# Copies of a bias made from DRAM to DRAM in an earlier layer, and rotary tables loaded into a free residual

## The chip, the cores and the metric

One core of a Trainium2 chip runs the whole program. TensorE (PE) multiplies, VectorE (DVE) and ScalarE (ACT) work on vectors, GpSimd (POOL) adds a little and issues some DMAs, SyncE (SP) issues most of the DMAs. The metric is the device time of one execution in microseconds.

## The reference

Two blocks of a network follow each other for 256 positions of width 1024. Block 1 is one layer of dilated attention and a state space scan with a feed-forward part. Block 2 has two layers on two streams, the target `x` and a context `xc`. Each layer is a feed-forward part, a mixer over both streams and a second feed-forward part. The mixer of layer 1 joins a latent attention (MLA) with rotary positions and a neighbourhood attention whose scores get a bias per head and per distance:

```python
for l in range(DEPTH_2):
    ...
    x = x + 0.5 * mx[2] * swiglu_2(modulate(rms_norm(x), mx[0], mx[1]), *ffn1)
    xc = xc + 0.5 * mc[2] * swiglu_2(modulate(rms_norm(xc), mc[0], mc[1]), *ffn1)
    h = modulate(rms_norm(x), mx[3], mx[4])
    hc = modulate(rms_norm(xc), mc[3], mc[4])
    ...            # l == 0: window and differential attention, l == 1: the one below
    x = x + mx[5] * y
    x = x + 0.5 * mx[8] * swiglu_2(modulate(rms_norm(x), mx[6], mx[7]), *ffn2)

# in mix_mla_neighbourhood (layer 1)
q_rope = apply_rope2d(rms_norm(q[..., C_NOPE:], qn_rope), cos, sin)
k_rope = apply_rope2d(rms_norm(k_rope, kn_rope), cos, sin)
# in neighbourhood_attention, for each of the 4 rows of 64 positions
bias = rpb_f[:, dr_idx[None, :, None], dc_idx[:, None, :]]
s = jnp.einsum('bqhd,bjkhd->bhqjk', q_row, k_band).astype(jnp.float32) * scale + bias
```

After layer 1's mixer the context is not needed any more, so its residual is last read by the norm ahead of that mixer.

## The kernel before

Activations lie with the features on the 128 partitions, as eight blocks of 128 x 256 for each stream. A linear unit multiplies one 128-wide slab of a weight matrix (512 KB, loaded by SP into one of five `wraw` buffers at L107) with all eight blocks. Weights and activations are each split into two parts (`wh`, `wl` by L114 and L115; `ah`, `al` by L355 and L356), and three products of the parts make one in full precision (L133 to L135). `K.run` goes through a list of units and emits loads and splits some units ahead; plain functions in the list, such as `tables`, are emitted where they stand, and `weave` spreads a list of such steps evenly between units. The order in which an engine takes its instructions is planned by the framework from the data that they need; each engine's queue is then fixed and is worked off in order.

A norm of a stream (`norm_stream`, with raised priority) is a chain: sums over PE (L330), mean on DVE (L314), root on ScalarE (L315), reciprocal on DVE (L316), spreading over PE (L338), and then for each block a product on DVE (L351), a cast with the shift on ScalarE (L355) and the remainder on DVE (L356).

The mixer of layer 1 is `mix_cd`. Its units are, in order: two of `cd_ckv` (indices 0 and 1), six of `cd_cq` for the target alone, one of `cd_kr` (index 8), four of `cd_dk` (9 to 12) and others. At its beginning ScalarE's queue loads the rotary tables `cos` and `sin` (96 x 256 each, L1397 and L1398) into temporary buffers, and `tables`, behind unit 4, scales them by the gains of queries and keys (L1093, L1094) into blocks 4 to 7 of `free`, the place of the context's residual `xc`. POOL's queue loads the bias rows of eight heads (889 elements each, `A["rpb"][:, 4:11]`) onto eight partitions of blocks 0 to 3 of `free` (L1402), and then writes 64 copies of them to the DRAM tensor `rpb` (L1404), from which the neighbourhood attention later reads a bias per head that is shifted by one element from row to row:

```python
    rows = free[:8, 0:4].rearrange("p a t -> p (a t)")[:, :7 * 127]
    nc.gpsimd.dma_start(rows, A["rpb"][:, 4:11].rearrange("h r c -> h (r c)"))
    rpb = K.dram.tile([64, 8, 7 * 127], F32, name="rpb")
    nc.gpsimd.dma_start(rpb.rearrange("q h u -> h q u"), rows.unsqueeze(1).to_broadcast([8, 64, 7 * 127]))
```

The same pattern stands at the start of block 1: the bias rows `brs` of eight partitions are written as 32 copies to the DRAM tensor `brow` (L474, 896 KB), and the load of `tri` (L478) and two mask loads `mk` (L500) stand behind it in the code. POOL's only arithmetic is the addition of a mask to the bias in the neighbourhood attention (L1597).

In layer 0, `block2` weaves 40 steps into the units of the first feed-forward part. Each step is one piece of the modulation (`K.pieces`): a load of 512 KB (`w_mod`) and two products on DVE (L981).

Of the kernel before, what the change touches and what calls it, by code (L numbers as in the profile page):

```python
# [8 lines left out]
F32 = mybir.dt.float32  # L9
# [1081 lines left out]
def rope_tables(K, c, s, cos, sin, gain, gain_sw, scale, rows):  # L1091
    nc = K.nc
    nc.vector.tensor_scalar(c[rows], cos[rows], gain[rows], scale, op0=ALU.mult, op1=ALU.mult)  # L1093
    nc.vector.tensor_scalar(s[rows], sin[rows], gain_sw[rows], scale, op0=ALU.mult, op1=ALU.mult)  # L1094
    return c[rows], s[rows]
# [8 lines left out]
def skew(work):  # L1104

    deep, out = max(len(w) for w in work), []
    for i in range(len(work) + deep - 1):
        for d in range(deep):
            if 0 <= i - d < len(work) and d < len(work[i - d]):
                out.append(work[i - d][d])  # L1110
    return out
# [17 lines left out]
def v_units(K, src, n, kpb, evac, last):  # L1129

    nc = K.nc
    nsl = -(-KB // kpb)

    def make(i):
        def f(s, slabs):
            for t in range(2):
                if t:
                    K.step()

                p = (K.pa.tile([128, 512], F32, name="pa") if i == last else K.psum())[:, :n]  # L1140
                for k in range(KB):
                    h, lo = slabs[k // kpb]
                    c = slice(k % kpb * n, (k % kpb + 1) * n)
                    ah, al = K.ACT[s][0][:, k, t * 128:(t + 1) * 128], K.ACT[s][1][:, k, t * 128:(t + 1) * 128]
                    nc.tensor.matmul(p, ah, h[:, c], start=k == 0, stop=False)  # L1145
                    nc.tensor.matmul(p, al, h[:, c], start=False, stop=False)
                    nc.tensor.matmul(p, ah, lo[:, c], start=False, stop=k == KB - 1)  # L1147
                evac(s, t, i, p)
        return Unit(src, i * nsl, nsl, f)

    return [make(i) for i in range(src.shape[0] // nsl)]


def out_proj(K, src, layer, streams, done, steps=()):
    def evac(m):
        return lambda s, p: K.residual(s, m, p, K.mod(layer, s, 5)(m), True)

    K.run(weave([K.lin(src, m, K.acts, evac(m)) for m in range(KB)], steps), streams, done=done)
# [232 lines left out]
def mix_cd(K, streams):  # L1391
    nc, A = K.nc, K.A
    ctx = ExitStack()
    ap = K.pool(ctx, "cd", 1)
    full, r96 = slice(0, 128), slice(0, 96)
    cos, sin = K.t1("cos"), K.t1("sin")
    nc.scalar.dma_start(cos[r96], A["mla_cos"])  # L1397
    nc.scalar.dma_start(sin[r96], A["mla_sin"])  # L1398
    sw_mask = [p ^ 8 for p in range(32)]
    free = K.X["c"]  # L1400
    rows = free[:8, 0:4].rearrange("p a t -> p (a t)")[:, :7 * 127]
    nc.gpsimd.dma_start(rows, A["rpb"][:, 4:11].rearrange("h r c -> h (r c)"))  # L1402
    rpb = K.dram.tile([64, 8, 7 * 127], F32, name="rpb")
    nc.gpsimd.dma_start(rpb.rearrange("q h u -> h q u"), rows.unsqueeze(1).to_broadcast([8, 64, 7 * 127]))  # L1404
    tabs = {}

    def tables():
        for n, k, at_ in (("q", "cq", 4), ("k", "ckr", 6)):
            c, s = rope_tables(K, free[:, at_], free[:, at_ + 1], cos, sin, K.col(k), K.col(k + "_sw"), 1.0, r96)
            tabs[n] = (c, s, sw_mask)  # L1410

    dqg = ap.tile([128, 1], F32, name="dqg")
# [25 lines left out]
    def latent(kind, b):  # L1438
        def evac(s, p):
            k = (kind, s)  # L1440
            nc.scalar.copy(raw[k][:, b], p)
            K.square_add(kind + s, raw[k][:, b], b == 0)
            if b + 1 == rank[k]:
                K.later(lambda: first(k))

        def first(k):
            r = K.rstd_cols(K.sums(k[0] + k[1]), 2, 1.0 / (128 * rank[k]), 1e-6)
            K.later(lambda: second(k, r))

        def second(k, r):  # L1450
            q = K.on_all(r)
            n = range(rank[k])
            K.norm(k[0], [raw[k][:, j] for j in n], lambda j: K.col("cq_a" if kind == "q" else "ckv_a", j), None,
                   *([t[:, j] for j in n] for t in parts[k]), q)

        return evac
# [58 lines left out]
    units = [K.lin(A["cd_ckv"], b, K.acts, latent("k", b)) for b in range(2)]  # L1515
# [6 lines left out]
    dq_units = [K.lin(A["cd_dq"], b, K.acts, dq_evac(b), streams=one) for b in range(4)]  # L1522
    units += dq_units[:2] + [vc_unit(i) for i in range(2)] + dq_units[2:]
    units += v_units(K, A["cd_dv"], 256, 4, vd_evac, 1)
    K.run(units[:5] + [tables] + units[5:-1], streams, ko=2)
    K.flush()
    tctx.close()

# [82 lines left out]
    steps = skew(work + [attend(b, scores_d, 1.0, vd, 4 + b) for b in range(4)])  # L1611
# [6 lines left out]
    ctx.close()  # L1618


def block2(K, layers=(0, 1)):
    nc, A = K.nc, K.A
    for layer in layers:
        both = ["c", "x"]

        def norms(i, layer=layer):
            return lambda s: K.norm_stream(s, K.mod(layer, s, i + 1), K.mod(layer, s, i))

        fctx = ExitStack()
        hid_p = K.pool(fctx, "h1", 14)  # L1630
        K.ffn(A[f"f1g{layer}"], A[f"f1u{layer}"], [A[f"f1d{layer}{i}"] for i in range(3)], both,
              lambda s, m: K.mod(layer, s, 2)(m), hid_p, K.pieces(40), norms(3))
        fctx.close()
        K.dbg(f"d_xf{layer}", K.X["x"])
        K.dbg(f"d_cf{layer}", K.X["c"])
        if layer == 0:
            mix_ab(K, both)
            out_proj(K, A["ab_out"], 0, both, norms(6))
            tail = both
        else:  # L1640
            while K.bg:
                K.background()
            K.mctx.close()
            mix_cd(K, both)
            out_proj(K, A["cd_out"], 1, ["x"], norms(6))
            tail = ["x"]
        K.dbg(f"d_xm{layer}", K.X["x"])
        K.dbg(f"d_cm{layer}", K.X["c"])
        fctx = ExitStack()
        hid_p = K.pool(fctx, "h2", 14)  # L1650

        def done(s):
            K.norm_stream(s, K.mod(1, s, 1), K.mod(1, s, 0))

        def after(s, m):
            if layer == 1:
                nc.sync.dma_start(A["out"][:, m], K.X["x"][:, m])

        K.ffn(A[f"f2g{layer}"], A[f"f2u{layer}"], [A[f"f2d{layer}{i}"] for i in range(3)], tail,
              lambda s, m: K.mod(layer, s, 8)(m), hid_p, K.pieces(40 if layer == 0 else 0),  # L1660
              done if layer == 0 else None, after)
        fctx.close()
        K.dbg(f"d_x2{layer}", K.X["x"])
# [3 lines left out]
def kernel(ctx, tc, A, parts=(1, 2)):  # L1667
# [24 lines left out]
    if 2 in parts:  # L1692
        for s in ("c", "x") if 1 not in parts else ():
            for b in range(KB):
                K.square_add(s, K.X[s][:, b], b == 0)
            K.norm_stream(s, K.mod(0, s, 1), K.mod(0, s, 0))
        block2(K)
    else:
        K.flush()
        nc.sync.dma_start(A["out"], K.X["x"])  # L1700
# [189 lines left out]
```

## Time and profile before

| | us |
|---|---|
| median of 3 runs | 2549.88 |
| lowest and highest run | 2544.33 and 2550.07 |
| the profiled execution | 2545.32 |
| its span, first to last instruction | 2543.5 |

Busy time is given for each engine; operations on one engine overlap a little at their ends. A row of a timeline gives the start, the duration, the engine, the line, the operation with its output and inputs and how many were merged, and in brackets the idle time of the engine before it and what ended that. ACTq and SPq are the queues of ScalarE and SP on which they issue DMAs. q0 is the DMA queue of POOL, q1 that of SP, and a queue's share is the time of its packets as a part of the time of all 16 DMA engines.

### The profile page before, as it was taken

What the parts mean: (1) busy time and instruction counts of PE and PEld (TensorE: products, weight loads), DVE (VectorE), ACT (ScalarE), POOL (GpSimd) and SP (SyncE); (2) the same over time, 40 slices, a digit from 0 to 9 for tenths busy, and PEclk for the clock granted to TensorE, in tenths of its full rate; (3) what the DMA queues carried; (4) which work ended last, traced back from release to release, by engine and by line L of the source; (5) the groups of instructions that cost most, each with busy time, mean ns of one, the idle gap of its engine ahead of it and who ended that gap; (6) DMA issues with size and microseconds to landing.
All of it is one profiled execution on the core that took longest, in us unless ns stands there. A gap on an engine that the chain in (4) does not pass through costs nothing.

```text
span 2543.5 us, 38370 instructions
## 1 busy us (share of the span) xinstructions
PE 2457.1 (97%) x15104; PEld 2122.3 (83%) x15104; DVE 1642.2 (65%) x3009; ACT 1070.2 (42%) x1934; POOL 15.4 (1%) x20
## 2 busy tenths in 40 slices
PE   6999999999999999999999999999999968999999
PEld 6999999999988888885598888888888857866999
DVE  4667777787867564767767666566545344667554
ACT  4657565535522222436743222243222234555443
POOL 0000000000000000000000000000000000000000
PEclk9999899999999999999999999999999988999999
DMA  8555455676455553431025545325555342232563
GB/s 227 148 156 161 144 163 182 210 246 203 162 166 167 164 168 99 130 98 51 1 75 178 170 150 170 128 91 178 171 166 164 103 96 74 98 95 82 172 185 125
DMA packets 117204, 363.66 MB, mean 143 GB/s; under 512 B 21050, under 2 KB 28730, under 8 KB 117024
## 3 DMA queue, kind: packets, MB, share of 16 engines
q1 hardware_dynamic: 114512, 355.73, 44.2%
q0 software_dynamic: 1008, 3.09, 1.0%
q10 hardware_dynamic: 1504, 2.40, 0.3%
q8 instruction: 119, 1.95, 0.3%
q14 instruction: 61, 0.50, 0.1%
HBM read 357.34 MB, written 3.82 MB: 142 GB/s over the span
## 4 chain that ended last, share of the span: by engine, by line
PE 70%; DVE 2%; DMA 2%; ACT 1%; issue 0%; ACTq 0%
PE pm L133 20%; PE pm L134 20%; PE pm L135 20%; PE pt L1120 1%; DMA sin<-mla_sin 1%; PE pa L1027 1%; PE pt L1051 1%; PE pa L1574 1%; PE pm L1319 1%; PE pm L1582 1%; PE pm L1259 0%; PE pa L1335 0%; PE pa L1296 0%; PE pm L1604 0%; PE pm L1145 0%; PE pa L1147 0%
## 5 line engine op out<-in xcount | busy, mean ns | idle before, releaser
L133 PE MATMUL pm<-ah,wh 128*128 128x256 f32 (+2 forms) x3096 | 1012.7, 329 | 46.4 <-ACT ah L355 35.6
L134 PE MATMUL pm<-al,wh 128*128 128x256 f32 (+2 forms) x3096 | 1007.1, 326 | 1.2 <-DVE al L356 1.1
L135 PE MATMUL pm<-ah,wl 128*128 128x256 f32 (+2 forms) x3096 | 1005.2, 325 | 0.0
L114 ACT CAST wh<-wraw 128x1024 fp32r<-128x1024 f32 (+4 forms) x535 | 540.3, 1013 | 1057.1 <-PE pm L134 850.0
L115 DVE TENSOR_TENSOR wl<-wraw,wh 128x1024 fp32r<-128x1024 f32 (+4 forms) x535 | 627.2, 1175 | 242.2 <-ACT wh L114 240.0
L133 PEld LDWEIGHTS pm<-ah,wh 128*128 128x128 f32 (+1 forms) x3096 | 588.6, 191 | 107.2 <-ACT ah L355 37.3
L134 PEld LDWEIGHTS pm<-al,wh 128*128 128x128 f32 (+1 forms) x3096 | 590.7, 191 | 54.2 <-issue 2.4
L135 PEld LDWEIGHTS pm<-ah,wl 128*128 128x128 f32 (+1 forms) x3096 | 590.6, 191 | 51.4 <-issue 1.7
L134 PE MATMUL pm<-hl,wh 128*128 128x512 f32 (+1 forms) x934 | 317.1, 339 | 0.0
L133 PE MATMUL pm<-hh,wh 128*128 128x512 f32 (+1 forms) x934 | 316.6, 339 | 0.0
L135 PE MATMUL pm<-hh,wl 128*128 128x512 f32 (+1 forms) x934 | 316.4, 339 | 0.0
L981 DVE SCALAR_TENSOR_TENSOR junk<-wraw,cactc 128x1024 f32<-128x1024 f32 x112 | 137.2, 1225 | 213.2 <-DMA wraw<-w_mod 212.8
L981 DVE SCALAR_TENSOR_TENSOR junk<-wraw,cactx 128x1024 f32<-128x1024 f32 x144 | 176.0, 1222 | 41.0 <-DMA wraw<-w_mod 38.6
L133 PEld LDWEIGHTS pm<-hh,wh 128*128 128x128 f32 x934 | 175.9, 188 | 21.2 <-issue 0.2
L135 PEld LDWEIGHTS pm<-hh,wl 128*128 128x128 f32 x934 | 175.9, 188 | 20.9
L134 PEld LDWEIGHTS pm<-hl,wh 128*128 128x128 f32 x934 | 175.9, 188 | 20.9
L119 ACT CAST hh<-g 128x512 fp32r<-128x512 f32 (+1 forms) x113 | 59.2, 526 | 162.1 <-DVE g L413 162.1
L413 DVE TENSOR_TENSOR g<-g,pm 128x512 f32<-128x512 f32 (+1 forms) x113 | 64.0, 566 | 58.7 <-PE pm L135 57.3
L120 DVE TENSOR_TENSOR hl<-g,hh 128x512 fp32r<-128x512 f32 (+1 forms) x113 | 63.8, 566 | 0.3
L409 ACT ACTIVATE g<-pm 128x512 f32<-128x512 f32 (+1 forms) x116 | 56.1, 489 | 2.5 <-PE pm L135 2.3
L443 DVE SCALAR_TENSOR_TENSOR xc<-pm,mcol0c,xc 128x256 f32<-128x256 f32 x56 | 26.9, 480 | 46.0 <-PE pm L135 45.8
L307 DVE TENSOR_TENSOR acc<-acc,sq 128x256 f32<-128x256 f32 x105 | 42.3, 419 | 13.7 <-ACT sq L306 13.4
(421 smaller groups left out, 2228.7 us busy)
## 6 DMA issues: line engine op xcount, KB each, us to landing
wraw<-w_mod SPq DMA_DIRECT2D x144, 512.0 KB, 4.1
wraw<-f1g SPq DMA_DIRECT2D x44, 512.0 KB, 3.7
wraw<-f1u SPq DMA_DIRECT2D x44, 512.0 KB, 4.2
wraw<-f2g SPq DMA_DIRECT2D x44, 512.0 KB, 3.7
wraw<-f2u SPq DMA_DIRECT2D x44, 512.0 KB, 4.0
wraw<-f1d SPq DMA_DIRECT2D x32, 512.0 KB, 4.0
wraw<-f2d SPq DMA_DIRECT2D x32, 512.0 KB, 3.7
wraw<-w_xbc SPq DMA_DIRECT2D x24, 512.0 KB, 3.6
```

The costliest lines, as they stand in the source:

```text
L114: nc.scalar.copy(h[:, :f], raw[:, :f])
L115: nc.vector.tensor_tensor(lo[:, :f], raw[:, :f], h[:, :f].bitcast(F32), op=ALU.subtract)
L119: self.nc.scalar.copy(h, src)
L120: self.nc.vector.tensor_tensor(lo, src, h.bitcast(F32), op=ALU.subtract)
L133: nc.tensor.matmul(out, h[:, c], ah, start=first, stop=False)
L134: nc.tensor.matmul(out, h[:, c], al, start=False, stop=False)
L135: nc.tensor.matmul(out, lo[:, c], ah, start=False, stop=last)
L307: nc.vector.tensor_tensor(self.acc[key], self.acc[key], sq, op=ALU.add)
L409: nc.scalar.activation(half(g["g"], s), p, AF.Silu)
L413: nc.vector.tensor_tensor(t, t, p, op=ALU.mult)
L443: self.nc.vector.scalar_tensor_tensor(x, p, gate, x, op0=ALU.mult, op1=ALU.add)
L981: nc.vector.scalar_tensor_tensor(junk, raw, 1.0, K.cact[s], op0=ALU.mult, op1=ALU.mult, accum_out=K.mcol[layer, s][:, j:j + 1])
```

## The change

The copies of the bias are made by eight DMAs, each of 8 x 8 rows straight from the input in DRAM to the DRAM tensor. They are emitted as steps 10 to 17 of the list that layer 0 weaves into its first feed-forward part, which then has 48 steps. They stand on POOL's queue as before. The load of the rows into `free` and the broadcast store in `mix_cd` go away. The rotary tables are loaded twice, as four DMAs on POOL's queue, straight into blocks 4 to 7 of `free`, and are scaled there in place. `tables` stands behind unit 8 and no longer behind unit 4.

```diff
--- before.py
+++ after.py
@@ -1393,20 +1393,17 @@
     ctx = ExitStack()
     ap = K.pool(ctx, "cd", 1)
     full, r96 = slice(0, 128), slice(0, 96)
-    cos, sin = K.t1("cos"), K.t1("sin")
-    nc.scalar.dma_start(cos[r96], A["mla_cos"])
-    nc.scalar.dma_start(sin[r96], A["mla_sin"])
     sw_mask = [p ^ 8 for p in range(32)]
     free = K.X["c"]
-    rows = free[:8, 0:4].rearrange("p a t -> p (a t)")[:, :7 * 127]
-    nc.gpsimd.dma_start(rows, A["rpb"][:, 4:11].rearrange("h r c -> h (r c)"))
-    rpb = K.dram.tile([64, 8, 7 * 127], F32, name="rpb")
-    nc.gpsimd.dma_start(rpb.rearrange("q h u -> h q u"), rows.unsqueeze(1).to_broadcast([8, 64, 7 * 127]))
+    for i, n in enumerate(("cos", "sin", "cos", "sin")):
+        nc.gpsimd.dma_start(free[r96, 4 + i], A["mla_" + n])
+    rpb = K.rpb
     tabs = {}
 
     def tables():
         for n, k, at_ in (("q", "cq", 4), ("k", "ckr", 6)):
-            c, s = rope_tables(K, free[:, at_], free[:, at_ + 1], cos, sin, K.col(k), K.col(k + "_sw"), 1.0, r96)
+            c, s = free[:, at_], free[:, at_ + 1]
+            c, s = rope_tables(K, c, s, c, s, K.col(k), K.col(k + "_sw"), 1.0, r96)
             tabs[n] = (c, s, sw_mask)
 
     dqg = ap.tile([128, 1], F32, name="dqg")
@@ -1522,7 +1519,7 @@
     dq_units = [K.lin(A["cd_dq"], b, K.acts, dq_evac(b), streams=one) for b in range(4)]
     units += dq_units[:2] + [vc_unit(i) for i in range(2)] + dq_units[2:]
     units += v_units(K, A["cd_dv"], 256, 4, vd_evac, 1)
-    K.run(units[:5] + [tables] + units[5:-1], streams, ko=2)
+    K.run(units[:9] + [tables] + units[9:-1], streams, ko=2)
     K.flush()
     tctx.close()
 
@@ -1618,6 +1615,13 @@
     ctx.close()
 
 
+def bias_rows(K):
+
+    K.rpb = K.dram.tile([64, 8, 7 * 127], F32, name="rpb")
+    rows = K.A["rpb"][:, 4:11].rearrange("h r c -> h (r c)").unsqueeze(0).to_broadcast([8, 8, 7 * 127])
+    return [lambda i=i: K.nc.gpsimd.dma_start(K.rpb[8 * i:8 * i + 8], rows) for i in range(8)]
+
+
 def block2(K, layers=(0, 1)):
     nc, A = K.nc, K.A
     for layer in layers:
@@ -1626,10 +1630,13 @@
         def norms(i, layer=layer):
             return lambda s: K.norm_stream(s, K.mod(layer, s, i + 1), K.mod(layer, s, i))
 
+        steps = K.pieces(40)
+        if layer == 0:
+            steps[10:10] = bias_rows(K)
         fctx = ExitStack()
         hid_p = K.pool(fctx, "h1", 14)
         K.ffn(A[f"f1g{layer}"], A[f"f1u{layer}"], [A[f"f1d{layer}{i}"] for i in range(3)], both,
-              lambda s, m: K.mod(layer, s, 2)(m), hid_p, K.pieces(40), norms(3))
+              lambda s, m: K.mod(layer, s, 2)(m), hid_p, steps, norms(3))
         fctx.close()
         K.dbg(f"d_xf{layer}", K.X["x"])
         K.dbg(f"d_cf{layer}", K.X["c"])
```

## Rows read from the trace of the kernel before

**Rows 1.** The page, part 1: busy time of each engine, share of the span.

```profile
PE 2457.1 (97%) x15104; PEld 2122.3 (83%) x15104; DVE 1642.2 (65%) x3009; ACT 1070.2 (42%) x1934; POOL 15.4 (1%) x20
```

**Rows 2.** Stretches: us, busy per engine (instructions), granted clock, DMA share, GB/s.

```profile
1050.00:1055.00 5.00, 5.00 (x30) 5.00 (x30) 3.06 (x11) 0.91 (x2) 0.00 (x0) 0.62 0.00 2
2074.90:2106.60 31.70, 1.84 (x8) 1.78 (x8) 3.14 (x11) 2.92 (x10) 0.00 (x0) 0.55 0.56 88
```

**Rows 3.** Timeline of DVE around the tables: start, us, operation, idle before.

```profile
2070.33 0.87 DVE L351 SCALAR_TENSOR_TENSOR y<-xc,mcol1c,pt 128x256 f32<-128x256 f32 x2
...
2075.21 0.15 DVE L314 TENSOR_SCALAR v<-pt 128x2 f32<-128x2 f32 x1
...
2079.31 0.16 DVE L316 RECIPROCAL rs<-rs 128x2 f32<-128x2 f32 x1
2097.09 0.35 DVE L1093 TENSOR_SCALAR xc<-cos,cols 96x256 f32<-96x256 f32 x1 [17.63 <-DMA cos<-mla_cos]
2105.04 0.35 DVE L1094 TENSOR_SCALAR xc<-sin,cols 96x256 f32<-96x256 f32 x1 [7.60 <-DMA sin<-mla_sin]
...
2105.57 1.25 DVE L351 SCALAR_TENSOR_TENSOR y<-xx,mcol1x,pt 128x256 f32<-128x256 f32 x3
```

**Rows 4.** Timeline of PE at the same place.

```profile
2106.64 1.22 PE L133 MATMUL pm<-ah,wh 128*128 128x256 f32 x4 [25.19 <-ACT ah L355]
```

**Rows 5.** Timeline of ScalarE at the same place (ACTq: its DMA issues).

```profile
2073.50 4.27 ACTq L1398 DMA_DIRECT2D sin<-mla_sin  x1
...
2078.84 0.19 ACT L315 ACTIVATE rs<-v 128x2 f32<-128x2 f32 x1
```

**Rows 6.** DMA from 2071.4 to 2111.2: queue; issues, KB each, us to landing.

```profile
q0 software_dynamic: 528, 1.82, 42.9%
...
rpb<-xc POOLq DMA_DIRECT2D x1, 1778.0 KB, 39.7
wraw<-cd_cq SPq DMA_DIRECT2D x1, 512.0 KB, 26.0
```

**Rows 7.** DMA over the whole span: issues, KB each, median us to landing.

```profile
wraw<-cd_cq SPq DMA_DIRECT2D x6, 512.0 KB, 3.5
...
mk<-mask POOLq DMA_DIRECT2D x2, 64.0 KB, 4.7
...
xc<-rpb POOLq DMA_DIRECT2D x1, 27.8 KB, 2.1
```

**Rows 8.** Timeline of DVE and PE at the same transition in layer 0.

```profile
1042.85 0.16 DVE L316 RECIPROCAL rs<-rs 128x2 f32<-128x2 f32 x1
...
1046.69 0.80 PE L133 MATMUL pm<-ah,wh 128*128 128x256 f32 x3 [1.59 <-ACT ah L355]
```

**Rows 9.** Timeline of POOL over the span.

```profile
2.46 0.57 POOL L478 DMA_DIRECT2D tri<-tri  x1
11.04 0.71 POOL L474 DMA_DIRECT2D brow<-brs  x1 [8.01 <-DVE brs L473]
...
2069.05 0.53 POOL L1402 DMA_DIRECT2D xc<-rpb  x1 [2035.69 <-ACT ah L355]
```

**Rows 10.** Timeline of DVE at the start.

```profile
1.00 0.06 DVE L946 MEMSET one<- 128x1 f32 x1
```

**Rows 11.** Feed-forward 1 of layer 0: DMA queue of SP, and the stretch.

```profile
q1 hardware_dynamic: 13838, 49.35, 48.6%
...
690.00:1010.00 320.00, 320.00 (x1378) 259.38 (x1377) 198.67 (x304) 83.02 (x102) 0.00 (x0) 1.00 0.49 155
```

**Rows 12.** Stretches of the start.

```profile
0.00:40.00 40.00, 20.83 (x120) 17.49 (x121) 21.27 (x42) 19.28 (x33) 3.78 (x10) 0.92 0.79 227
8.00:10.00 2.00, 2.00 (x5) 0.28 (x3) 1.90 (x6) 1.22 (x6) 0.00 (x0) 1.00 1.03 411
```

**Rows 13.** DMA issues from 11.5 to 13 us.

```profile
wraw<-w_k SPq DMA_DIRECT2D x1, 512.0 KB, 20.2
```

**Rows 14.** DMA from 2538 us to the end, stores of the output: queue.

```profile
q1 hardware_dynamic: 288, 0.26, 13.5%
```

## Prediction

> **What bounds the kernel now.** I read the page first: TensorE (PE) is busy for 97% of the span [rows 1], so a change can give back time only where PE stands still. The table of stretches shows the largest such place: from 2074.9 to 2106.6 us, 31.7 us, PE works for 1.84 us [rows 2]. The timeline of VectorE (DVE) names the reason: it waits 17.63 us for the cosine table and 7.60 us for the sine table. In the same rows the reader sees what is queued behind: the reciprocal of the target's norm is done at 2079.31 + 0.16, and the first product of that norm (L351), which PE needs for its next block, starts only at 2105.57 [rows 3]. PE restarts at 2106.64 after 25.19 us without an operand [rows 4]. ScalarE's timeline adds a smaller piece: the issue of the sine load alone holds its queue for 4.27 us, and the root of the same norm, whose input v was there at 2075.21 + 0.15 = 2075.4 [rows 3], runs at 2078.84 [rows 5].
>
> Why are two loads of 96 KB late? The DMA view of that stretch answers it: the copy rpb<-xc (8 source partitions, 512 rows of 3556 bytes, queue q0) takes 39.7 us, and beside it a 512 KB weight load takes 26.0 us [rows 6]; the median of the same matrix's loads is 3.5 [rows 7]. So the flood of bias copies starves all other loads for 40 us.
>
> **What the change takes away.** The flood leaves this place, and the two table loads leave ScalarE's queue. The new restart of PE follows from R, the end of the reciprocal. The root comes right behind v: 2075.4 + 0.2, then the reciprocal 0.16 [rows 3, 5]: R = 2075.8. From R to PE's restart the spreading of the norm over PE, the first L351 and the first cast remain. From below, the last two alone took 2106.64 - 2105.57 = 1.1 us [rows 3, 4]. From above, the same transition in layer 0, whose DVE does small work and tables in between, took from 1042.85 to 1046.69, 3.8 us [rows 8]. The middle is 2.5: PE restarts at 2078.3, a gain of 28 us, with bounds 27 and 29.7. PE's clock gives nothing more: its mean was 0.55 in the stretch (nearly all of it at the lower level of 1.2 GHz), and in layer 0, where PE stood for only a short wait (1.59 us, rows 8), it still was 0.62 in five us after the restart, part of them at that level [rows 2].
>
> **The four new loads.** They stand on GpSimd's (POOL's) queue, and blocks 4 to 7 of the context's residual must first have been read: the last L351 on it ends at 2070.33 + 0.87 = 2071.2 [rows 3]. Four issues of some 0.55 us [rows 9] end by 2074. A load from POOL landed after 2.1 us in quiet and 4.7 us beside the start's traffic [rows 7]: the last lands between 2076 and 2078.7. Behind them on POOL stand only the bias additions of the attention, much later. The four table operations take 0.35 us each [rows 3]; they are emitted later than before, but DVE took three of them ahead of the target's norm before, and may again. That L351 could start at 2078.3 - 1.1 = 2077.2, so the cost is 0 if they stand behind it, and at most 1.5 + 1.4 = 2.9 us if all stand ahead. I take 0: layer 0's row, on which the middle above rests, has tables ahead of the norm. Scaling in place costs DVE the same four operations. Two temporary buffers come free earlier; no row shows a wait for one here, so nothing.
>
> **The eight copies: where they run.** They read an input and write a scratch tensor of their own, so nothing makes them wait, and POOL has nothing to do for 2035.69 us before L1402 [rows 9]. That the loop puts them between units of layer 0 does not hold them there. The rows show instructions without inputs taken early: the memset of `one`, written behind the whole mixer of block 1, runs at 1.00 us [rows 10], and on POOL itself the load of tri (L478) is issued at 2.46, ahead of the earlier line L474, which waits for data until 11.04 [rows 9]. So I expect the copies on POOL from about 3 us, ahead of brow.
>
> **What they cost there.** Nothing in layer 0's feed-forward: its PE is busy 320.00 of 320 us with DMA at 0.49 [rows 11]. The eight places that they take among the modulation steps press those together by at most 48/40, and DVE's 198.67 of 320 us becomes at most 0.75 of a stretch: hidden. But in the first 40 us PE works only 20.83 us, and the DMA engines are full, 1.03 at 411 GB/s between 8 and 10 us [rows 12]: there the loads of x and of the first weights set when PE starts. A flood starves them here as it does later: during brow's copy a weight load takes 20.2 us [rows 13]. The trace shows no copy from DRAM to DRAM. From below: a packet of weights costs 0.486 x 16 x 320 / 13838 = 0.18 engine-us for 3.6 KB [rows 11], and one of the output's stores 0.135 x 16 x 5.5 / 288 = 0.041 for 0.9 KB [rows 14], as fast per byte. From above: rpb<-xc took 0.429 x 16 x 39.8 / 528 = 0.52 for 3.4 KB [rows 6], read from eight partitions. Reading DRAM and writing DRAM are both in the lower rows, so I take 0.18: 512 rows are 92 engine-us, 5.8 us over 16 engines. The upper price is 265, 16.6 us over 16 engines or 33 over 8. Since the copies go ahead of x's last blocks and of brow, I charge all of the 5.8, as 6 us; the bound below is 0. If they held brow back for longer, the bias loads on SP's queue, which wait for brow, would add to that.
>
> **The sum.** 2545.3 (profiled execution; span 2543.5) - 28 + 6 = 2523. The median of the runs, 2549.9, lies 4.6 above that execution; between 2523 and 2528 I say 2525. A measurement here tells about 0.3%, 7.6 us, from no change.
>
> **Rivals.**
> (a) The copies stay in layer 0, or the start hides them. For it: POOL has room at any time. Against: the rows of tri and `one`, and the full DMA engines of the start. 2545.3 - 28 = 2517. Chance 0.15.
> (b) Half of the engines carry the copies. For it: rpb<-xc, whose outer dimension is 8 like that of each copy, left the DMA share at 0.56 [rows 2], some eight engines beside the loads. Against: eight separate copies need not all take the same eight. Then 64 rows of 0.18 on each, 11.5 us: 2529 from the profiled execution, 2533 from the median. Chance 0.2. The Trainium skill, DMA: Bandwidth & Descriptors, section Rules for kernel authors, states that an outermost dimension below 16 confines a DMA to at most that many engines. The trace agrees with it in the 0.56 of rows 2; by it 11.5 us takes the place of 5.8 unless the copies take turns, and the sum would be 2529.
> (c) The other side: slower. Place: POOL's queue between tri and brow. Price: each row as dear as in rpb<-xc, on the same eight engines, 64 x 0.52 = 33 us, so 2545.3 - 28 + 33 = 2550, from the median's level 2555. Against the gain it decides from 28 / 64 = 0.44 us a row on. For it: the only copies of such rows in the trace ran at that rate, on the same queue. Against: their source was eight partitions. Chance 0.12; a little over half of that ends slower by 0.3%.
> (d) The table wait stays in part: loads late or tables ahead of the norm, 2.9 us back: 2526 to 2531. Chance 0.1.
>
> **How the numbers follow.** The forecast itself, 2517 to 2531, has 0.43. Faster by over 0.3%: forecast, (a), (b) and (d), 0.88, less 0.03 for what no row shows (another order of instructions elsewhere): 0.85. Slower: 0.07, from (c); within 0.3%: 0.08, the rest of (c) and those 0.03. The range runs from the full gain at the lowest run, 2544 - 29 = 2515, to copies at 16.6 us at the median's level, 2550 - 27 + 17 = 2540; what lies outside is (c) and a sliver of (a).
>
> **What would show it.** Right: DVE's two waits for tables gone; ScalarE's root within 1 us of v; PE's wait ahead of L133 at this place 1 to 4 us instead of 25; the eight copies on POOL's timeline before 15 us; PE's first block later by some 6 us. Wrong: copies at 700 us or later (then a); the first weights or brow late by 20 us or more (then c); a wait of L1093 or L1094 for a DMA of several us (then d).

## The result and the profile after

The changed kernel takes 2520.2 us (median of 4 runs, 2518.77 to 2521.83); the kernel before, beside it, took 2549.98 (4 runs). The ratio is 0.989, 95% interval 0.987 to 0.991: faster by 1.1%; the medians lie 29.8 us apart. The profiled execution is 2521.26 us against 2545.32 before, 24.1 less. Two later sets of runs gave 2525.66 (ratio 0.990, 0.988 to 0.992) and 2521.55 (0.988, 0.986 to 0.990).

The page, its first lines and the line of POOL's DMA queue (packets, MB, share):

```profile
span 2519.5 us, 38382 instructions
...
PE 2459.8 (98%) x15104; PEld 2122.6 (84%) x15104; DVE 1642.6 (65%) x3009; ACT 1069.2 (42%) x1934; POOL 20.6 (1%) x30
...
q0 software_dynamic: 1280, 3.45, 0.7%
```

PE's busy time is that of [rows 1] within 3 us, and the span is 24 us shorter: PE stands still for less time, and does the same work. POOL's queue moves more than before (3.45 MB, where the page of before has 3.09) in a smaller share of the engines' time (0.7%, where it has 1.0%). Where PE gains its time, the timelines of the stretch of [rows 3 to 5] show: DVE, then ScalarE, then PE.

```profile
2075.46 0.14 DVE L1410 TENSOR_SCALAR dqg<-cols 128x1 f32<-128x1 f32 x1
...
2077.73 0.16 DVE L314 TENSOR_SCALAR v<-pt 128x2 f32<-128x2 f32 x1 [0.49 <-PE pt L330]
2077.80 1.22 DVE L115 TENSOR_TENSOR wl<-wraw,wh 128x1024 fp32r<-128x1024 f32 x1
2078.94 0.16 DVE L316 RECIPROCAL rs<-rs 128x2 f32<-128x2 f32 x1
...
2079.33 0.34 DVE L1093 TENSOR_SCALAR xc<-xc,cols 96x256 f32<-96x256 f32 x1
2079.60 0.34 DVE L1094 TENSOR_SCALAR xc<-xc,cols 96x256 f32<-96x256 f32 x1
2079.96 1.26 DVE L351 SCALAR_TENSOR_TENSOR y<-xx,mcol1x,pt 128x256 f32<-128x256 f32 x3
...
2077.92 0.20 ACT L315 ACTIVATE rs<-v 128x2 f32<-128x2 f32 x1
...
2079.24 0.68 PE L338 MATMUL pt<-ident,rs 128*128 128x128 f32 x4 [1.55 <-DVE rs L316]
...
2081.04 1.22 PE L133 MATMUL pm<-ah,wh 128*128 128x256 f32 x4 [0.78 <-ACT ah L355]
```

The two waits for tables are gone: L1093 and L1094 have no bracket. The root follows v within 0.2 us. PE waits 1.55 us for the spreading (L338) and 0.78 us for the first cast. Before, it waited 25.19 us for the cast [rows 4], and for the spreading this long:

```profile
2079.61 1.19 PE L338 MATMUL pt<-ident,rs 128*128 128x128 f32 x4 [4.73 <-DVE rs L316]
```

Together that is 29.9 us before and 2.3 after, 27.6 less. What the reader should also see is the `wl` of 1.22 us between v and the reciprocal: DVE now has other work ready there.

POOL's timeline shows where the copies and the table loads went:

```profile
2.48 0.58 POOL L478 DMA_DIRECT2D tri<-tri  x1
3.06 0.60 POOL L1622 DMA_DIRECT2D rpb<-rpb  x1
11.47 0.69 POOL L474 DMA_DIRECT2D brow<-brs  x1 [7.82 <-DVE brs L473]
12.15 0.57 POOL L1622 DMA_DIRECT2D rpb<-rpb  x1
34.38 1.15 POOL L500 DMA_DIRECT2D mk<-mask  x2 [21.66 <-DMA brow<-brs]
35.50 3.41 POOL L1622 DMA_DIRECT2D rpb<-rpb  x6
2072.34 0.53 POOL L1399 DMA_DIRECT2D xc<-mla_cos  x1 [2033.44 <-ACT ah L355]
...
2074.72 0.51 POOL L1399 DMA_DIRECT2D xc<-mla_sin  x1
```

None of the eight copies ran in layer 0. One stands ahead of brow, one behind it, and six behind the masks. At the start PE and ScalarE lose some two microseconds; the rows of before come first, then those of after:

```profile
37.76 0.58 PE L133 MATMUL pm<-ah,wh 128*128 128x256 f32 x1 [8.24 <-ACT q L526]
...
32.58 1.04 ACT L114 CAST wh<-wraw 128x1024 fp32r<-128x1024 f32 x1 [11.24 <-DMA wraw<-w_k]
```

```profile
39.93 0.58 PE L133 MATMUL pm<-ah,wh 128*128 128x256 f32 x1 [8.33 <-ACT q L526]
...
34.93 2.13 ACT L114 CAST wh<-wraw 128x1024 fp32r<-128x1024 f32 x2 [12.13 <-DMA wraw<-w_k]
```

To split the span, I take six marks, each at the start of its first instruction: the load of `w_z` (a weight of block 1), the sum `xx<-pm,one,xx` on DVE (block 1's feed-forward part adds its first result to the residual; called xx), the load of `ab_out` (the projection behind layer 0's mixer), `dqg` (the DVE row above), the load of `cd_out` (the projection behind layer 1's mixer) and the store of the output. Microseconds between marks, for two profiles of before and three of after:

| stretch | before | before, again | after | after, again | after, third |
|---|---|---|---|---|---|
| start to w_z | 168.1 | 167.3 | 170.7 | 170.3 | 171.6 |
| w_z to xx | 357.4 | 357.8 | 350.9 | 353.4 | 350.7 |
| xx to ab_out (holds layer 0's first feed-forward) | 581.7 | 580.8 | 581.1 | 582.5 | 580.9 |
| ab_out to dqg | 965.4 | 969.9 | 972.8 | 969.7 | 966.9 |
| dqg to cd_out (the place of the wait) | 144.6 | 143.8 | 118.0 | 116.3 | 116.3 |
| cd_out to output | 308.3 | 309.8 | 307.9 | 308.1 | 308.2 |
| output to end | 18.0 | 18.2 | 18.1 | 18.1 | 18.1 |
| span | 2543.5 | 2547.6 | 2519.5 | 2518.4 | 2512.7 |

By the means, the place of the wait is 144.2 - 116.9 = 27.3 us shorter and the start 170.9 - 167.7 = 3.2 us longer, together 24.1. The mean spans differ by more, 28.7 us. Most of the rest lies in two stretches: w_z to xx is 5.9 us shorter after the change and ab_out to dqg 2.2 longer. Both follow the granted clock (see the last section), and the first is no property of the change as far as the runs show: the next run, with the same copies, has 359.3 us there. The start is not exact to a microsecond either: in the six profiles below and above that have no copies there, w_z comes at 166.9 to 169.5 us.

### The profile page after: what moved, and what is told of

Read it like the earlier page. It is cut to its first block, busy times and chain, and to the rows that moved or that the text cites. A ratio compares the mean times of both kernels' runs of the same rounds, so it can differ in the third digit from the quotient of the medians.

```text
span 2519.5 us, 38382 instructions
## 1 busy us (share of the span) xinstructions
PE 2459.8 (98%) x15104; PEld 2122.6 (84%) x15104; DVE 1642.6 (65%) x3009; ACT 1069.2 (42%) x1934; POOL 20.6 (1%) x30
## 3 DMA queue, kind: packets, MB, share of 16 engines
q0 software_dynamic: 1280, 3.45, 0.7%
## 4 chain that ended last, share of the span: by engine, by line
PE 71%; DVE 2%; ACT 1%; issue 0%; DMA 0%; ACTq 0%
PE pm L133 21%; PE pm L134 21%; PE pm L135 20%; PE pt L1120 1%; PE pm L1319 1%; PE pa L1027 1%; PE pt L1051 1%; PE pa L1571 1%; PE pa L1335 1%; PE pm L1579 1%; PE pm L1259 0%; PE pa L1296 0%; PE pm L1601 0%; PE pm L1145 0%; PE pa L1147 0%; PE pa L1145 0%
## 5 line engine op out<-in xcount | busy, mean ns | idle before, releaser
L1120 PEld LDWEIGHTS pt<-ident,e 128*128 128x128 f32 x272 | 30.7, 144 | 21.8 <-issue 18.7
```

The source lines that it names most:

```text
L1120: nc.tensor.transpose(p[:, j * 128:(j + 1) * 128], b, K.ident)
```

## The experiments

Each ratio is to the kernel before on the same chip, with its 95% interval. Each diff is against the change, only that of the cheap copies at the old place against the kernel before; `...` marks what is left out.

**The copies alone.** The change's copies, with the tables on ScalarE's queue, unit 4 and `cos`, `sin` as before.

```diff
+    cos, sin = K.t1("cos"), K.t1("sin")
+    nc.scalar.dma_start(cos[r96], A["mla_cos"])
+    nc.scalar.dma_start(sin[r96], A["mla_sin"])
...
-    for i, n in enumerate(("cos", "sin", "cos", "sin")):
-        nc.gpsimd.dma_start(free[r96, 4 + i], A["mla_" + n])
...
-    K.run(units[:9] + [tables] + units[9:-1], streams, ko=2)
+    K.run(units[:5] + [tables] + units[5:-1], streams, ko=2)
```

> The eight copies as in the change; the table loads, their buffers and the place of the scaling as before it (ScalarE's queue, temporary buffers, behind unit 4). Theory A, the flood beside the table loads was the cause: both tables land within 4 us, DVE waits for them 2 us at most, PE waits under 5 us at this place, profiled time 2519 to 2524 (the changed kernel: 2521.3). Theory B, the queue and the place of the tables was the cause: ScalarE's issue of 4 us and a DVE wait of 10 us or more stay, 2535 or more.

Measured: 2525.08 us (7 runs), ratio 0.991 (0.989 to 0.994). The wait is gone with the old table loads in place:

```profile
2086.59 1.23 PE L133 MATMUL pm<-ah,wh 128*128 128x256 f32 x4 [1.65 <-ACT ah L355]
```

The start is that of the change (w_z at 170.7). The profiled time, 2535.3, misses the expected 2519 to 2524: from 2175 to 2190 us PE was busy 15.00 of 15 us at a granted clock of 0.50, and from 250 to 270 it was busy throughout at 0.65 (last section). The tables' way into the residual thus adds nothing that these runs can tell.

**The tables alone.** The change's tables; the bias rows, their broadcast store and the 40 steps as before.

```diff
+    rows = free[:8, 0:4].rearrange("p a t -> p (a t)")[:, :7 * 127]
+    nc.gpsimd.dma_start(rows, A["rpb"][:, 4:11].rearrange("h r c -> h (r c)"))
+    rpb = K.dram.tile([64, 8, 7 * 127], F32, name="rpb")
+    nc.gpsimd.dma_start(rpb.rearrange("q h u -> h q u"), rows.unsqueeze(1).to_broadcast([8, 64, 7 * 127]))
     for i, n in enumerate(("cos", "sin", "cos", "sin")):
...
-        if layer == 0:
-            steps[10:10] = bias_rows(K)
```

> The four table loads on GpSimd's queue and the scaling in place as in the change; the flood of 512 rows from eight partitions stays in layer 1, planned behind the table loads. Theory A1, only the tables suffered from the flood: PE restarts as early as in the changed kernel, the weight loads land 25 to 36 us late but five units are split ahead, PE waits 0 to 6 us for weights, and the start costs nothing: 2517 to 2524. Theory A2, the flood only finds its next victim: PE waits 10 to 20 us for the weights of the next units, 2530 to 2540. Theory C, the new loads or places give nothing: 2543 or more.

Measured: 2529.25 us (10 runs), ratio 0.993 (0.991 to 0.995), between the expected outcomes. PE goes on at 2076.20, but the flood of copies finds its next victim 25 us later. ScalarE's rows of the timeline:

```profile
2100.93 1.05 ACT L114 CAST wh<-wraw 128x1024 fp32r<-128x1024 f32 x1 [7.77 <-DMA wraw<-cd_dk]
...
2111.10 1.04 ACT L114 CAST wh<-wraw 128x1024 fp32r<-128x1024 f32 x1 [8.40 <-DMA wraw<-cd_dk]
```

PE's row in the view of waits over the whole run (us in total, times, longest; the longest is at this place):

```profile
PE pt L330 <- DVE acc L307: 16.3, 5, 9.1
```

Two lines of the DMA view from 2070 to 2120 us (KB each, median us to landing):

```profile
wraw<-cd_dk SPq DMA_DIRECT2D x4, 512.0 KB, 23.8
rpb<-xc POOLq DMA_DIRECT2D x1, 1778.0 KB, 41.1
```

The weights of `cd_dk` take 23.8 us each, and PE stands for 9.1 us once. From dqg to cd_out it is 127.6 us: of the 27.3 us to be gained, 10.7 are given back. Loading the tables ahead of the flood moves part of the wait to the next loads; it does not remove its cause.

**The copies really in layer 0.** The rows pass through a tile that comes free only there, are stored once to DRAM, and the eight copies read that.

```diff
-    rows = K.A["rpb"][:, 4:11].rearrange("h r c -> h (r c)").unsqueeze(0).to_broadcast([8, 8, 7 * 127])
-    return [lambda i=i: K.nc.gpsimd.dma_start(K.rpb[8 * i:8 * i + 8], rows) for i in range(8)]
+    one = K.dram.tile([8, 7 * 127], F32, name="rpb1")
+
+    def first():
+        t = pool.tile([8, 7 * 127], F32, name="rowst", bufs=1)
+        K.nc.gpsimd.dma_start(t, K.A["rpb"][:, 4:11].rearrange("h r c -> h (r c)"))
+        K.nc.gpsimd.dma_start(one, t)
+
+    rows = one.unsqueeze(0).to_broadcast([8, 8, 7 * 127])
+    return [first] + [lambda i=i: K.nc.gpsimd.dma_start(K.rpb[8 * i:8 * i + 8], rows) for i in range(8)]
```

> As the change, but the copies really run in layer 0: the 8 rows are first loaded into a tile that comes free there, stored to DRAM once, and copied eight times from that. Theory: the 2.6 us that the first 180 us lost come from the two copies ahead of and beside brow; here the first 180 us are those of the kernel before, layer 0 hides the copies, profiled time 2518 to 2520. Rival: the copies cost in layer 0 what they cost at the start, or the loss at the start has another cause: 2521 or more.

Measured: 2523.25 us (5 runs), ratio 0.990 (0.987 to 0.994). POOL issues the copies in layer 0:

```profile
671.90 4.01 POOL L1629 DMA_DIRECT2D rpb<-rpb  x8 [3.48 <-DMA rpb<-rowst]
```

They cost nothing there (xx to ab_out 581.1 us, as in the table), and the start is free of them: w_z at 166.9 against 170.3 to 171.6. The profiled time, 2524.9, misses the expected 2518 to 2520 and lies where the rival put it, but not by the rival's cause: neither the start nor layer 0 is longer, and from w_z to xx it is 364.1 us, with PE busy 20.00 of 20 us at a clock of 0.50 from 250 to 270. The 4 us at the start are too few to be told by the medians.

**The change's order, but read from eight partitions.** The copies are issued at the same places in POOL's order (one ahead of brow, one behind it, six behind the masks), with the rows of a tile of eight partitions as their source.

```diff
         nc.gpsimd.dma_start(masks[-1], A[f"mask{g}"])
+    bias_rows(K, ct)
...
-    rows = K.A["rpb"][:, 4:11].rearrange("h r c -> h (r c)").unsqueeze(0).to_broadcast([8, 8, 7 * 127])
-    return [lambda i=i: K.nc.gpsimd.dma_start(K.rpb[8 * i:8 * i + 8], rows) for i in range(8)]
+    t = t[:8].rearrange("p a t -> p (a t)")[:, :7 * 127]
+    K.nc.gpsimd.dma_start(t, K.A["rpb"][:, 4:11].rearrange("h r c -> h (r c)"))
+    rows = t.unsqueeze(1).to_broadcast([8, 8, 7 * 127])
+    for i in range(8):
+        K.nc.gpsimd.dma_start(K.rpb[8 * i:8 * i + 8].rearrange("q h u -> h q u"), rows)
```

> As the change, with the same order on GpSimd's queue, but each copy reads its rows from eight partitions of a tile in SBUF. Theory: the source on eight partitions makes a row dear (0.5 engine-us a packet on q0, 0.2 from DRAM): the copies behind the masks take some 30 us, starve the weight and bias loads from 35 to 70 us, and PE loses 5 to 15 us there: 2526 to 2536. Rival: the row costs the same from either source and only the place of the flood mattered: within 1.5 us of the changed kernel.

Measured: 2548.61 us (10 runs), ratio 1.000 (0.999 to 1.002): the whole gain is gone, more than was expected. The place of the wait is as good as in the change (118.0 us), and w_z comes at 196.2, 25.5 later than in the change's profile. The DMA view from 38 to 80 us:

```profile
q0 software_dynamic: 600, 1.56, 55.9%
...
rpb<-ct POOLq DMA_DIRECT2D x6, 222.2 KB, 19.1
wraw<-w_v SPq DMA_DIRECT2D x2, 512.0 KB, 23.8
```

A stretch of it (us, busy per engine, clock, DMA share, GB/s):

```profile
60.00:80.00 20.00, 7.89 (x65) 7.48 (x64) 4.07 (x4) 5.31 (x8) 0.00 (x0) 0.83 1.01 170
```

The queue's packets took 0.559 x 16 x 42 = 376 engine-us (us of one of the 16 DMA engines) for 1.56 MB. A queue's packets are of very unequal size, so I divide by bytes: 0.86 engine-us for a row of 3556 bytes. In the change, from 35.5 to 45 us, where the same six copies run:

```profile
q0 software_dynamic: 488, 1.46, 45.3%
...
rpb<-rpb POOLq DMA_DIRECT2D x6, 222.2 KB, 7.0
```

That is 0.453 x 16 x 9.5 = 69 engine-us for 1.46 MB, or 0.17 for a row. The same copies, the same queue and the same order: the source makes a factor of five.

**All eight copies ahead of brow.** The order that the prediction took for granted, with the change's source.

```diff
     brow = K.dram.tile([32, 8, 896], F32, name="brow")
+    for f in bias_rows(K):
+        f()
...
-        if layer == 0:
-            steps[10:10] = bias_rows(K)
```

> As the change, but all eight copies are written ahead of the broadcast of brow and stand there on GpSimd's queue, as the prediction assumed them to. Theory, the prediction's price (0.18 engine-us a packet, 5.8 us over 16 engines, all of it ahead of x and brow): the first load of w_z comes at 174 us, 6 later than before the change (168.1) and 3.3 later than after it (170.7). Rival: a copy costs less than that where it waits for its turn beside the loads, 172 or less; or as much as from eight partitions, 190 or more.

Measured: 2528.67 us (4 runs), ratio 0.991 (0.989 to 0.993). w_z comes at 179.2, 11.5 later than the mean of before, where the prediction charged 6. POOL, then PE:

```profile
2.47 3.40 POOL L1624 DMA_DIRECT2D rpb<-rpb  x6
...
16.61 0.67 POOL L476 DMA_DIRECT2D brow<-brs  x1 [8.45 <-DVE brs L475]
...
33.00 1.22 PE L133 MATMUL pm<-ah,wh 128*128 128x256 f32 x4 [9.02 <-ACT ah L119]
```

The copies hold back x (6.9 us to landing instead of 5.0), with it the first norm, and so brow, which starts 5.6 us later than in [rows 9]; the weights then stand beside brow (w_q 16.5 us, w_k 18.3). So the change's cheap start depends on its order: six copies stand where PE already works.

**Cheap copies at the old place.** The kernel before in everything else; the rows are stored once to DRAM and copied from there, in layer 1.

```diff
-    nc.gpsimd.dma_start(rpb.rearrange("q h u -> h q u"), rows.unsqueeze(1).to_broadcast([8, 64, 7 * 127]))
+    rpb1 = K.dram.tile([8, 7 * 127], F32, name="rpb1")
+    nc.gpsimd.dma_start(rpb1, rows)
+    for i in range(8):
+        nc.gpsimd.dma_start(rpb[8 * i:8 * i + 8], rpb1.unsqueeze(0).to_broadcast([8, 8, 7 * 127]))
```

> As the kernel before, at the same place in layer 1, with one edit: the rows go from the eight partitions to DRAM once, and the 64 copies are made from that, DRAM to DRAM. Theory P, the price of a row is the cause, not the place: the copies take 5 to 10 us instead of 40, the tables land within 8 us, DVE waits for them 5 us at most, the start costs nothing: profiled time 2517 to 2523. Rival, any flood at this place holds the tables back: 2535 or more.

Measured: 2518.37 us (4 runs), ratio 0.989 (0.986 to 0.991). POOL, DVE and PE:

```profile
2072.78 4.20 POOL L1407 DMA_DIRECT2D rpb<-rpb  x8 [1.79 <-DMA rpb<-xc]
...
2076.68 0.39 DVE L1094 TENSOR_SCALAR xc<-sin,cols 96x256 f32<-96x256 f32 x1 [1.33 <-DMA sin<-mla_sin]
...
2078.31 1.22 PE L133 MATMUL pm<-ah,wh 128*128 128x256 f32 x4 [2.18 <-ACT ah L355]
```

The same 64 copies of the rows stand at the old place beside the old table loads. DVE waits 1.33 us for the sine instead of 7.60, and not at all for the cosine instead of 17.63; from dqg to cd_out it is 117.2 us, as in the change. Neither the move nor the tables is needed for the gain; the dear source was the cause of the wait. That there are eight DMAs here in place of one is not it: the copies read from eight partitions above were eight as well.

**brow the same way.** The copies held in layer 0 as above, and brow's 32 copies made from one stored row set.

```diff
-    nc.gpsimd.dma_start(brow.rearrange("q h u -> h q u"), brs.unsqueeze(1).to_broadcast([8, 32, 896]))
+    brow1 = K.dram.tile([8, 896], F32, name="brow1")
+    nc.gpsimd.dma_start(brow1, brs)
+    for i in range(4):
+        nc.gpsimd.dma_start(brow[8 * i:8 * i + 8], brow1.unsqueeze(0).to_broadcast([8, 8, 896]))
```

> As e3 (copies held in layer 0), and the broadcast of brow at the start too is made by one store and four copies from DRAM to DRAM. Theory P: the load that waited 20 us beside brow lands in 8 us, PE's wait of 8 us at 30 to 38 us falls below 2, the first load of w_z comes at 158 to 162 us, profiled time 2508 to 2514. Rival, the stall there has another cause than brow: first load of w_z within 2 us of 167, 2516 or more.

Measured: 2520.1 us (4 runs), ratio 0.988 (0.986 to 0.989). The expected gain at the start did not come: w_z at 168.9. The wait of 8 us at 38 us is gone, but what it gave is lost in the attention behind it:

```profile
20.00:75.00 55.00, 54.86 (x458) 54.15 (x456) 28.89 (x33) 24.14 (x38) 0.00 (x0) 1.00 0.70 210
75.00:80.00 5.00, 1.84 (x8) 1.36 (x9) 2.86 (x8) 4.21 (x11) 0.00 (x0) 0.92 0.56 169
80.00:85.00 5.00, 4.90 (x17) 2.67 (x18) 3.13 (x10) 2.31 (x9) 0.00 (x0) 0.50 0.97 200
85.00:90.00 5.00, 5.00 (x21) 3.24 (x22) 1.65 (x5) 1.19 (x5) 0.00 (x0) 0.50 0.00 0
```

PE stands 3.18 us for the probabilities of ScalarE (L582), and its clock falls behind that. In the change PE is busy 5.00 of each 5 us there at full clock. Why the linear units that fill this place there were used up here was not pursued.

**Cheap copies at the old place, with the change's tables.** Both ideas joined, with nothing added to the start: the diff is the one of the cheap copies at the old place, on top of the change's tables. Beside it ran the change and the kernel before once more.

> The kernel of e8 (bias rows stored once to DRAM, eight DRAM to DRAM copies in layer 1, nothing moved to the start) with the tables as in the change: four loads on POOL into blocks 4 to 7 of the context's residual, scaled in place. It joins the cheap row with a start that nothing was added to. Theory P (the dear source of the row was the cause, place hardly matters): the start is that of before, w_z first loaded at 167 to 168.5 us instead of 170.5; the four table loads are issued ahead of the copies, so DVE has no wait for a table; from dqg to the first cd_out load 115 to 118 us as in the change. Against the change's profiled 2519.5 that is 2 to 3 us, span 2515 to 2518 without a further dip of the clock, ratio to before 0.987 to 0.990: it can't be told from the change by the times. Rival (place matters: eight copies beside the first weights of layer 1 starve them as the 64 did): a wait of ACT on the first cd weights of 5 us or more, dqg to cd_out 122 or more, span 2522 or more.

> The change itself beside the run above on one chip, and a third profile of it. Expected: 2518 to 2526, ratio 0.988 to 0.992; w_z at 170 to 171; dqg to cd_out 116 to 118. The theory that the granted clock falls at places that change from one execution to the next expects dips at other times than 1235 to 1255 in this profile.

> A second profile of the kernel before. Every theory expects the wait of DVE for the tables as shown: dqg to the first cd_out load 143 to 146 us and w_z at 168. If instead dqg to cd_out differs by more than 3 us between the two profiles of before, the 26.6 us taken from one pair of profiles is no good measure of the gain. Dips of the clock are expected at other places than 255 to 270.

Measured: 2516.58 us (4 runs, 2514.44 to 2523.52), ratio 0.987 (0.985 to 0.989), the lowest of all, and not to be told from the change beside it (2521.55, 0.988, 0.986 to 0.990). w_z comes at 167.6 and dqg to cd_out is 117.9, as expected; the profiled span, 2521.7, is above the expected 2515 to 2518 and has two stretches of low clock (0.66 from 250 to 270 us and from 1235 to 1255). The two profiles of before agree on the wait within 0.8 us (144.6 and 143.8). The change once more, in an earlier set, had this expectation, and gave 2525.66 (6 runs):

> The changed kernel once more, for comparison on the same chip: 2519 to 2526, first load of w_z at 170 to 171 us.

## Why the prediction was right, and where its steps were not

**The gain (28 us, 27 to 29.7).** Measured 27.3. Its pieces: from v's end to PE's restart the prediction had 0.36 + 2.5 = 2.9 us; it was 2081.04 - 2077.89 = 3.15. The reciprocal did not follow v directly (1.05 us from v's end to its start, with `wl` between them), and from its end to the restart it was 1.94 instead of 2.5: two small misses of opposite sign. (The prediction's upper bound counts layer 0's 3.8 us from the reciprocal's start, not from its end; from its end it is 3.7.)

**The clock.** It gives nothing back, as said: in the five us behind the restart the mean was 0.50 and in the next five 0.88, in the change; before, it was 0.50 and 0.97. The row that the prediction took from layer 0 (0.62) starts 3.3 us behind the restart there; right behind it the mean was 0.53 for five us.

**The four table loads (0, at most 2.9).** They land in 2.1 to 2.3 us and no operation waits for them. Two of the four scalings stand ahead of the first L351 and take 0.6 us there, within the bound; but the spreading on PE (L338), which that L351 reads, ends only at 2079.92, and L351 starts at 2079.96. So the cost is 0.

**The place of the copies.** Right that layer 0 would not hold them; wrong that all eight would stand ahead of brow. The rows of `one` and tri show that an instruction without inputs is taken early; they do not show that eight of them in a row are. The planner put six behind the masks.

**The price of the copies (5.8 us, charged 6).** The price of a row, 0.18, was near: 0.17, and over 16 engines 5.4 us for all. The charge was mis-sized: 3.2 us measured. Two errors stand against each other in it. In the assumed order the eight cost 11.5 us, since a flood ahead of x delays a chain (x, norm, brow, weights) by more than its own transfer time; in the order that came, six of them run while PE is busy 5.00 of 5 us from 40 us on, and cost little. The sum, 2523 for the profiled time, was 2 us above the 2521.3 that came. That is partly luck: in this pair of profiles w_z to xx became 6.5 us shorter and ab_out to dqg 7.4 longer, mostly by the clock, and they cancelled.

**The rivals.** (a) half holds: the start hides six copies of eight. (b) does not hold for the change: from 40 to 42 us its copies had 63.4% of the time of all 16 engines, more than half. It does hold for the copies that are first stored to DRAM: joined with the change's tables they run alone on the queues from 2086 to 2092 us and stay at 51.7%, some eight engines. The change first, then that run:

```profile
q0 software_dynamic: 122, 0.48, 63.4%
...
q0 software_dynamic: 138, 1.28, 51.7%
```

The Trainium skill, DMA: Bandwidth & Descriptors, section Why a DMA increments its semaphore by 16 and not by 1, states that a POOL DMA of fewer than 16 shares takes consecutive engines from a cursor that moves on. The 63.4% agrees with copies that take turns in this way, the 51.7% does not, and no row here names the engines of one copy. Why the two differ stays open. (c) had its price right and its condition wrong: copies read from eight partitions at the start would have cost 196.2 - 167.7 = 28.5 us there, near its 33, and ended level with before. (d) didn't occur.

**The level.** The profile of before lay 4.6 us under its median, that of after 1.1 above its own; 2525 was put between the two levels, and the three medians, 2520.2, 2521.55 and 2525.66, lie from 4.8 below to 0.7 above it. Beside the medians of before they are 29.8, 29.3 and 25.5 us lower, where the forecast had 24.9 and the two stretches that the change touches give 24.1; the rest is in the stretches that follow the clock, and no term of the prediction.

## What to carry to other kernels

Look at what a flood reads before moving it: 64 copies of eight rows cost 0.5 to 0.9 engine-us a row read from eight partitions and some 0.15 read from DRAM, and one small store to DRAM ahead of the copies was worth the 1% by itself. A load that is issued ahead of a flood hands on part of the wait to the next loads (10.7 of 27.3 us here): look for the cause that all the late loads share. And a transfer at the start is charged by what stands behind it: the same eight copies cost 3 us when six of them stood behind the masks, and 11.5 when all stood ahead of the input.

## What the runs showed of the hardware

That DRAM to DRAM copies are this much cheaper than copies from eight partitions was no row of before. Loads beside the dear ones land late: 23.8 us for 512 KB (`w_v`), like the 26.0 in [rows 6]. Before the change both copies from eight partitions ran at one rate, some 45 GB/s: 1778 KB in 39.7 us [rows 6], and brow:

```profile
brow<-brs POOLq DMA_DIRECT2D x1, 896.0 KB, 20.6
```

The granted clock falls to its lower level (1.2 of 2.4 GHz) for 5 to 20 us at a few places, at some of them while PE is busy without a break. Whether it falls there, and for how long, changes from one execution to the next; the places recur. Two stretches of 20 us, first of before, then of after, then of the third profile of after:

```profile
250.00:270.00 20.00, 20.00 (x88) 16.14 (x89) 11.61 (x29) 4.83 (x10) 0.00 (x0) 0.66 0.18 56
1235.00:1255.00 20.00, 16.46 (x68) 9.50 (x68) 14.06 (x34) 16.63 (x32) 0.00 (x0) 0.83 0.00 0
```

```profile
250.00:270.00 20.00, 20.00 (x131) 16.60 (x130) 17.22 (x39) 8.32 (x16) 0.00 (x0) 1.00 0.21 67
1235.00:1255.00 20.00, 20.00 (x59) 11.41 (x58) 9.45 (x24) 11.39 (x24) 0.00 (x0) 0.52 0.00 0
```

```profile
250.00:270.00 20.00, 19.89 (x128) 16.34 (x127) 17.20 (x41) 8.32 (x17) 0.00 (x0) 1.00 0.22 71
1235.00:1255.00 20.00, 17.87 (x78) 10.34 (x77) 13.04 (x32) 16.68 (x36) 0.00 (x0) 0.85 0.00 1
```

At 250 us PE has no break in either of the first two, and 88 or 131 matmuls go through. Both profiles of before have the fall at 250 to 270 (0.66 and 0.67), two of the change's three do not, and the other has 0.83. From 1235 to 1255 all five have one: 0.83 and 0.66 before, 0.52, 0.66 and 0.85 after. There PE does pause first: just ahead of the fall it is busy for only 2.1 to 3.0 of five us in each of the five. The second profile of before and the third of the change expected the falls at other places than these, and that missed. A fall like the first costs (1 - 0.66) x 20 = 6.8 us by estimate, as the rows w_z to xx and ab_out to dqg of the table show. That is as large as the terms argued about here, and the reason to compare stretches between marks and not spans. Whether the kernel's edits shift the odds of a fall stays open.
